# A two-layer backbone kernel: order of the convolutions, buffers of the last attention unit, loads of the keys and of x, sums of the out projection

## The chip, the cores and the metric

The kernel runs on one core of one Trainium2 chip. Its time is the device time of one execution in microseconds (us). The engines are named as the profile names them: PE is TensorE (PEld its weight loads), DVE is VectorE, ACT is ScalarE, POOL is GpSimd, SP is the engine that issues most DMAs (SPq is its queue). All data are fp32.

## The reference

2048 latent tokens and 256 context tokens of width 1024 go through two layers. Both have the same frame:

```python
for layer in range(2):
    shift, scale, gate = adaln(c, w_ada[layer], b_ada[layer])     # and the same of c_ctx for the context
    h = rms_norm(x, g) * (1 + scale) + shift
    p = h @ w_in[layer]                                            # split into the columns of the mixer
    y = even_mixer(p, ...) if layer == 0 else odd_mixer(p, ...)
    x = x + gate * (y @ w_out[layer])
```

Layer 0 has two branches, each multiplied by the SiLU of its own gate columns. One is global attention: 8 query heads and 2 key heads of size 64, rotary embedding, normalised queries and keys, every query against 256 + 2048 keys. The other is a Hyena convolution over columns `u`, three parts of 512 channels: a short convolution of 3 taps on each part, then twice a long convolution (by transforms along the tokens) and a product. The context tokens go through the same with their own keys only, and their result feeds layer 1.

Layer 1 has windowed attention (each block of 128 queries against three blocks of 128 keys and the context, with a sink) and neighbourhood attention (8 by 16 keys around each query on the 64-wide grid, with a bias table), again with gates. Only the latent tokens are returned.

## The kernel before

**Projections.** Each fp32 factor is split into a high and a low part, so a product is three matmuls for each 128 rows of the sum (`mm3`, L216 to L221), 24 for one output tile of 128x512. Weights come in tiles of 128x512 (256 KB): `load_w` (L230) issues the DMA into a ring of three buffers `wraw`, ScalarE casts the high part `whi` (L242), and GpSimd computes the low part `wlo` (L243), which frees the buffer. The 2304 tokens are taken in three groups of 768 (`GRP`; the context is in group 0). `Proj.rows` computes tiles with tokens on the partitions and hands each to an evacuation (`ev_q` and `ev_kv` normalise, rotate, transpose into `tq` and store to the DRAM tensor `qk`; `ev_v`, L348, copies into a tile `vt` and stores that). `Proj.cols` computes tiles with columns on the partitions, among them the gates.

**Layer 0 up to attention** (L1296 to L1345). The adaLN products of both layers are summed in three PSUM banks with the tag "x" (`ada_sum`), of which the last is copied out by `ada_gates` (L114). Then follow the projections of the token groups and, in `latent_conv` (L704), the short convolutions of parts 0 and 1 of `u`: loads of columns from DRAM, one ScalarE and two VectorE operations on each half (L724 to L726), transposes into tiles of tag "x", and for part 0 the first transform `hpA` (L668), in tiles of the same tag. `gate_convs` (L680) does the short convolution of part 2 with one ScalarE and two VectorE operations (L697) on each of 16 tiles. The order in the code is

```python
us((0, 1))
conv(0)
us((2,))
conv(1)
gates((0,))
gate_convs(...)
```

where `us` computes columns of `u` for the last token group.

**Attention** (`glob_attn`, L907) runs 16 units (a block of 512 queries and a pair of heads) of 9 batches of two key tiles each: scores (L979, L980), exponential on ScalarE (L981), sums of P by GpSimd (`pacc`, L993), values into `po` (L998); maxima of the scores (`pm`, `mx`, L892 and L893) run a unit ahead. TensorE's order is written out by hand in this part (`manual_schedule`); `hooks` puts the steps of the long convolution into the early batches, opens the pools of the out projection behind them (`out_pools`), and puts 18 jobs of the out projection into the later ones. A unit's end is `yo` (copy of `po`, L1064), and two batches later `finish` (L1000): load of the gates `agt`, sums `pd`, copy into `rec`, four reciprocals of a quarter each, two products on GpSimd (L1015, L1016), and `finish_y` (L365), which splits y into `yhi` and `ylo` and stores both to `yT`. All these tiles are in the attention's pool, which closes before the pools of layer 1's projection (`hT1`, `ips1`, `s1`) open.

**Out projection** (`out_jobs`, L1377). A job is one tile of 128 tokens by 512 columns: 6 of group 0 in both halves of the columns and 6 of group 1 in one half run in attention, 6 and 12 more before the projections of layer 1's groups 1 and 2. A job loads its weights (the first of a half), y (two tiles `oy`), and x (`ox`, 0.5 MB, once for the two halves), and ends with

```python
t = rg.tile([P, 512], F32, tag="bo", name="ot", bufs=3)
V.tensor_tensor(out=t, in0=po, in1=gate, op=ALU.mult)
V.tensor_tensor(out=x, in0=x, in1=t, op=ALU.add)
```

**Layer 1** (L1492 to L1516). For each group: its out projection, its norm (transposes `lnpt`, `lnh`, halves of `hT`), rows of window keys and values, window queries, neighbourhood keys, queries and values, and the gate columns. In the last group `window_keys` (L1440) is called between the window queries and the neighbourhood keys: five loads of keys and values for all tokens (`wk`, `wv`), 4.7 MB, into a pool that has just been opened.

**Order.** Outside the hand-ordered part a planner walks a simulated timeline and takes on each engine, among the instructions that are ready there, the one that comes first in the code. SP's DMA issues are one queue in that order, and a waiting issue holds up those behind it.

Of the kernel before, what the change touches and what calls it, by code (L numbers as in the profile page):

```python
# [9 lines left out]
F32 = mybir.dt.float32  # L10
# [30 lines left out]
def kern(ctx, tc, nc, I, C, out):  # L41
# [207 lines left out]
    class Proj:  # L249
# [98 lines left out]
        def ev_v(self, dst):  # L348
            def f(ps, tt):
                vt = self.rg.tile([P, 512], F32, tag="bo", name="vt", bufs=3)  # L350
                S.copy(vt, ps)
                nc.sync.dma_start(dst[tt], vt)
            return f
# [11 lines left out]
    def finish_y(sb, y, ft, t0, n, yT=yT, tags=("yhi", "ylo"), bufs=2, eng=None):  # L365

        hi = sb.tile([P, 512], F32R, tag=tags[0], name="yhi", bufs=bufs)
        lo = sb.tile([P, 512], F32R, tag=tags[1], name="ylo", bufs=bufs)
# [538 lines left out]
    def glob_attn(sb, ps, hooks, M0):  # L907
# [92 lines left out]
        def finish(n, yo, acc):  # L1000

            qb, hp = units[n]
            gt = sb.tile([P, 512], F32, tag="agt", name="agt", bufs=1)
# [4 lines left out]
            rec = sb.tile([P, 512], F32, tag="rec", name="rec", bufs=1)  # L1008
# [9 lines left out]
            return [lambda i=i: quarter(i) for i in range(0, 512, 128)] + [gate, lambda: finish_y(sb, yo, hp, qb * 512, 512, bufs=1, eng=G)]  # L1018
# [3 lines left out]
        acc, po, ended, last, pend = {}, {}, {}, None, []  # L1022
        total = 16 * 41
# [9 lines left out]
        for b in range(nb + 4):  # L1033
# [23 lines left out]
            if last is not None:  # L1057
# [5 lines left out]
                if ks == 16:  # L1063
                    yo = sb.tile([P, 512], F32, tag="yo", name="yo", bufs=2)  # L1064
# [144 lines left out]
    with stS as st:  # L1209
# [109 lines left out]
        us((0, 1))  # L1319
# [6 lines left out]
        conv(0)  # L1326
        us((2,))
        conv(1)
# [52 lines left out]
    def out_jobs(g, halves, xs=None, early=()):  # L1381
# [9 lines left out]
        def job(b, i, tt, mm):  # L1391
            c = slice(512 * b, 512 * b + 512)
            rg, xo, gl = O0["rg"], O0["xo"], O0["gl"]
            if i == 0 and w_out.get("b") != b:
# [4 lines left out]
            ty = [xo.tile([P, 8, P], F32R, tag=f"oy{s}", name=f"oy{s}", bufs=2) for s in range(2)]  # L1399
            for s in range(2):  # L1400
                nc.sync.dma_start(ty[s].bitcast(F32), yT[s, :, :, tt * P:(tt + 1) * P].rearrange("f p t -> p f t"))
# [9 lines left out]
            else:  # L1411
                if len(xs) == i:
                    xt = xo.tile([P, 1024], F32, tag="lnx", name="ox", bufs=6)
                    if early:
# [9 lines left out]
            t = rg.tile([P, 512], F32, tag="bo", name="ot", bufs=3)  # L1424
            V.tensor_tensor(out=t, in0=po, in1=gate, op=ALU.mult)
            V.tensor_tensor(out=x, in0=x, in1=t, op=ALU.add)
# [13 lines left out]
    def window_keys():  # L1440
# [8 lines left out]
        wvt = aw.tile([P, 18, P], F32, tag="wv", name="wv")  # L1449
        for s in range(2):  # L1450
# [21 lines left out]

# [505 lines left out]
```

## Time and profile before

| | |
|---|---|
| Median of 3 runs | 3856.79 us (3853.07 to 3857.14) |
| Profiled execution | 3855.73 us, span of the trace 3854.0 us |
| TensorE matmuls | 3628.1 us, 94% of the span |
| TensorE weight loads | 2607.1 us, 68% |
| VectorE, ScalarE, GpSimd | 2284.9, 1784.9, 1735.3 us (59%, 46%, 45%) |
| DMA | 586.23 MB, mean 152 GB/s |

The span is the time from the first to the last recorded instruction, here 1.7 us less than the time of the same execution. Matmuls of one engine overlap in their pipeline, so the durations of rows of TensorE may add up to more than the time they take. A row of the timeline is a run of like instructions on one engine; the bracket at its end is the idle time of that engine just before it, and what ended it. Times on the left are counted from the start of the span, and the layers' parts lie in it as follows: layer 0's projections and convolutions up to 1080 us, attention up to 2254 us, layer 1's projections up to about 3080 us, then layer 1's attentions.

### The profile page before, as it was taken

How to read it: one execution, taken by the hardware profiler on the slowest of the kernel's cores; microseconds unless marked ns; L12 is line 12 of the kernel's file. 1: busy time of each engine (PE TensorE's matmuls, PEld its weight loads, DVE VectorE, ACT ScalarE, POOL GpSimd, SP SyncE). 2: the span in 40 equal slices, each digit the busy share in tenths (PEclk: the TensorE clock that was granted, in tenths of full speed). 3: DMA queues.
4: the chain of work that ended last, by engine and by line, in shares of the span. 5: the costliest groups of instructions: out<-in, count | busy, mean ns of one | idle time of the engine just before them, and what ended most of it. 6: DMA issues, size and time to landing. Idle time of an engine off the chain costs nothing.

```text
span 3854.0 us, 57179 instructions
## 1 busy us (share of the span) xinstructions
PE 3628.1 (94%) x20112; PEld 2607.1 (68%) x20112; DVE 2284.9 (59%) x4370; ACT 1784.9 (46%) x3480; POOL 1735.3 (45%) x1433
## 2 busy tenths in 40 slices
PE   6999999999779999999989989999999999999999
PEld 2788777666555544555545667778877888888887
DVE  5854862634967765776664348185168167677622
ACT  3644642423526655666452334344144266666610
POOL 1544642222447786777796554353244123222310
PEclk8999999999889999999999999999999999999999
DMA  6343445366666555443253545545566376365365
GB/s 195 118 140 123 133 133 141 114 224 219 203 191 189 172 162 173 123 148 110 91 197 96 146 148 152 164 152 155 157 175 169 118 171 147 90 151 135 113 178 169
DMA packets 537650, 586.23 MB, mean 152 GB/s; under 512 B 70590, under 2 KB 361720, under 8 KB 534290
## 3 DMA queue, kind: packets, MB, share of 16 engines
q1 hardware_dynamic: 521090, 551.10, 48.8%
q10 hardware_dynamic: 13856, 25.18, 1.8%
q0 software_dynamic: 2416, 6.29, 0.6%
q8 instruction: 159, 2.61, 0.3%
q14 instruction: 129, 1.06, 0.1%
HBM read 389.62 MB, written 192.75 MB: 151 GB/s over the span
## 4 chain that ended last, share of the span: by engine, by line
PE 69%; DVE 13%; issue 5%; DMA 5%; ACT 4%; POOL 2%; SPq 1%; ACTq 0%; DVEq 0%; POOLq 0%
PE psB L221 16%; PE pso L221 7%; PE po L998 6%; PE psA L221 5%; PE npt L1580 4%; PE no L1592 4%; PE pS L979 4%; PE pm L892 3%; PE pS L980 3%; PE ns L1561 2%; PE ns L1567 2%; DMA wraw<-in_w_in_dram 2%; PE hpX L806 1%; PE hpC L799 1%; PE hpH L811 1%
## 5 line engine op out<-in xcount | busy, mean ns | idle before, releaser
L243 POOL TENSOR_TENSOR wlo<-wraw,whi 128x512 fp32r<-128x512 f32 x368 | 494.4, 1357 | 784.9 <-ACT whi L242 529.3
L993 POOL TENSOR_TENSOR pacc<-pacc,Pt 128x512 f32<-128x512 f32 x512 | 647.1, 1286 | 191.4 <-ACT Pt L981 189.1
L221 PE MATMUL psB<-hT,whi 128*128 128x512 f32 (+1 forms) x2560 | 659.4, 346 | 3.9 <-DVE bo L341 3.5
L221 PE MATMUL psA<-whi,hT 128*128 128x512 f32 (+1 forms) x1952 | 574.8, 375 | 28.3 <-ACT vt L361 8.4
L893 DVE TENSOR_REDUCE mx<-pm 128x1 f32<-128x512 f32 (+1 forms) x640 | 389.1, 631 | 194.4 <-PE pm L892 190.1
L221 PEld LDWEIGHTS psB<-hT,whi 128*128 128x128 f32 x2560 | 445.1, 190 | 87.0 <-issue 23.9
L981 ACT ACTIVATE Pt<-pS 128x512 f32<-128x512 f32 x576 | 333.0, 597 | 352.5 <-PE pS L980 313.7
L221 PE MATMUL psB<-hT,wlo 128*128 128x512 f32 (+1 forms) x1280 | 433.8, 344 | 0.0
L221 PEld LDWEIGHTS psA<-whi,hT 128*128 128x128 f32 x1952 | 359.0, 194 | 98.7 <-ACT vt L361 11.7
L242 ACT CAST whi<-wraw 128x512 fp32r<-128x512 f32 x368 | 222.2, 618 | 301.4 <-DMA wraw<-in_w_in_dram 119.5
L221 PE MATMUL psA<-wlo,hT 128*128 128x512 f32 (+1 forms) x976 | 358.3, 372 | 0.9 <-POOL wlo L243 0.8
L221 PE MATMUL pso<-whi,oy 128*128 128x512 f32 x1088 | 343.2, 394 | 7.9 <-DMA oy<-yT 7.0
L979 PE MATMUL pS<-Q,K 128*128 128x512 f32 x576 | 330.9, 574 | 15.3 <-ACT Pt L981 14.9
L998 PE MATMUL po<-Pt,V 128*64 128x512 f32 x1152 | 283.0, 613 | 0.0
L221 PEld LDWEIGHTS psB<-hT,wlo 128*128 128x128 f32 x1280 | 242.4, 190 | 41.1 <-issue 10.8
L1580 PE MATMUL npt<-ident,np 128*128 128x128 f32 x1488 | 258.6, 283 | 3.4 <-DVE ggt L1157 1.9
L979 PEld LDWEIGHTS pS<-Q,K 128*128 128x128 f32 x576 | 109.7, 190 | 208.7 <-issue 95.3
L221 PEld LDWEIGHTS pso<-whi,oy 128*128 128x128 f32 x1088 | 205.2, 189 | 59.0 <-DMA oy<-yT 7.0
L980 PE MATMUL pS<-Q,K 65*128 65x512 f32 x576 | 231.3, 402 | 10.9 <-DMA Q<-mr 10.9
L892 PE MATMUL pm<-K,Q 128*128 128x512 f32 x600 | 217.0, 384 | 16.6 <-DVE mx L893 16.5
L221 PE MATMUL pso<-wlo,oy 128*128 128x512 f32 x544 | 213.2, 394 | 1.2 <-POOL wlo L243 1.2
L221 PEld LDWEIGHTS psA<-wlo,hT 128*128 128x128 f32 x976 | 189.9, 195 | 32.4 <-POOL wlo L243 3.1
(345 smaller groups left out, 6490.8 us busy)
## 6 DMA issues: line engine op xcount, KB each, us to landing
wraw<-in_w_in_dram SPq DMA_DIRECT2D x312, 256.0 KB
oy<-yT SPq DMA_DIRECT2D x72, 512.0 KB
qk<-tq SPq DMA_DIRECT2D x50, 512.0 KB
fA<-fev SPq DMA_DIRECT2D x64, 256.0 KB
adaw<-in_w_ada_dram SPq DMA_DIRECT2D x32, 512.0 KB
hxb<-XA SPq DMA_DIRECT2D x64, 256.0 KB
hfb<-fA SPq DMA_DIRECT2D x64, 256.0 KB
XC<-hevc ACTq DMA_DIRECT2D x64, 256.0 KB
```

What stands on the lines that cost most here:

```text
L221: T.matmul(ps, a(x, kt), b(y, kt), start=(kt == 0 and n == 0), stop=(kt == 7 and n == 2))
L242: S.copy(hi, w)
L243: G.tensor_tensor(out=lo, in0=w, in1=hi.bitcast(F32), op=ALU.subtract)
L892: T.matmul(pm[:, :n], self.q1[:, h, qt * P:(qt + 1) * P], self.K1(c0, n), start=True, stop=True)
L893: V.tensor_reduce(out=self.mx[:, u, c:c + 1], in_=pm[:, :n], axis=AX.X, op=ALU.max)
L979: T.matmul(s, K1[kv][:, kt * P:(kt + 1) * P], q1[:, h, :], start=True, stop=False)
L980: T.matmul(s, K2[kv][:, kt * P:(kt + 1) * P], q2[:, h, :], start=False, stop=True)
L981: S.activation(pt[:, h, :], s, AF.Exp)
L993: G.tensor_tensor(out=acc[1][:, h], in0=acc[1][:, h], in1=p[:, h], op=ALU.add)
L998: T.matmul(po[64 * h:64 * h + 64, :], vt[:, kt, kv * 64:kv * 64 + 64], p[:, h, :], start=(kt == 0), stop=(kt == 17))
L1580: T.transpose(pt[:, i, :], self.p[h][:, (i0 + i) * P:(i0 + i + 1) * P], ident)
L1592: T.matmul(B["po"][64 * h:64 * h + 64, self.k, :], vt[:, kt, 64 * h:64 * h + 64], self.pT[h, i // 4][:, i % 4, :], start=(i == 0), stop=(i ...
```

## The change

Five edits. (1) `us((1,))` moves behind `conv(0)`, and `us((2,))` behind `conv(1)`. (2) For the last unit of attention (15), `agt`, `rec`, `yo`, `yhi` and `ylo` are taken from three tiles of the out projection's y ring (`last_home`), when the values of its last batch are done. (3) The five loads of window keys are issued after the rows of neighbourhood values, and held by copies of one column from the last `vt` into each of the three tiles. (4) A job's loads of y come ahead of its weights, and from the third job of group 0 on the load of x is held by a copy of one column from the x two jobs back. (5) The product with the gate is written back to the PSUM tile, and the sum with x reads it there; tile `t` goes.

```diff
         def ev_v(self, dst):
             def f(ps, tt):
-                vt = self.rg.tile([P, 512], F32, tag="bo", name="vt", bufs=3)
+                vt = self.late = self.rg.tile([P, 512], F32, tag="bo", name="vt", bufs=3)
                 S.copy(vt, ps)
                 nc.sync.dma_start(dst[tt], vt)
...
-    def finish_y(sb, y, ft, t0, n, yT=yT, tags=("yhi", "ylo"), bufs=2, eng=None):
-        hi = sb.tile([P, 512], F32R, tag=tags[0], name="yhi", bufs=bufs)
-        lo = sb.tile([P, 512], F32R, tag=tags[1], name="ylo", bufs=bufs)
+    def finish_y(sb, y, ft, t0, n, yT=yT, tags=("yhi", "ylo"), bufs=2, eng=None, home=None):
+        hi = home[0] if home else sb.tile([P, 512], F32R, tag=tags[0], name="yhi", bufs=bufs)
+        lo = home[1] if home else sb.tile([P, 512], F32R, tag=tags[1], name="ylo", bufs=bufs)
         S.copy(hi[:, :n], y)
         (eng or V).tensor_tensor(out=lo[:, :n], in0=y, in1=hi[:, :n].bitcast(F32), op=ALU.subtract)
...
-    def glob_attn(sb, ps, hooks, M0):
+    def glob_attn(sb, ps, hooks, M0, last_home):
...
         def finish(n, yo, acc):
             qb, hp = units[n]
-            gt = sb.tile([P, 512], F32, tag="agt", name="agt", bufs=1)
+            tail = iter(home[0]) if n == 15 else None
+            gt = next(tail) if tail else sb.tile([P, 512], F32, tag="agt", name="agt", bufs=1)
             nc.sync.dma_start(gt, g0[hp, :, qb * 512:qb * 512 + 512])
             pd = ps.tile([P, 512], F32, tag="m", name="pd", bufs=3)
             for h in range(2):
                 T.matmul(pd[64 * h:64 * h + 64, :], ones[:, 64:P], acc[:, h, :], start=True, stop=True)
-            rec = sb.tile([P, 512], F32, tag="rec", name="rec", bufs=1)
+            rec = next(tail) if tail else sb.tile([P, 512], F32, tag="rec", name="rec", bufs=1)
             S.copy(rec, pd)
             def quarter(i):
...
                 G.tensor_tensor(out=rec, in0=rec, in1=gt, op=ALU.mult)
                 G.tensor_tensor(out=yo, in0=yo, in1=rec, op=ALU.mult)
-            return [lambda i=i: quarter(i) for i in range(0, 512, 128)] + [gate, lambda: finish_y(sb, yo, hp, qb * 512, 512, bufs=1, eng=G)]
+            return [lambda i=i: quarter(i) for i in range(0, 512, 128)] + [gate, lambda: finish_y(sb, yo, hp, qb * 512, 512, bufs=1, eng=G, home=home[1] if tail else None)]
         acc, po, ended, last, pend = {}, {}, {}, None, []
+        home = []
...
                 for i in range(2):
                     values(m, ks + i, tiles[i], po[m])
                 if ks == 16:
-                    yo = sb.tile([P, 512], F32, tag="yo", name="yo", bufs=2)
+                    if m == 15:
+                        home[:] = last_home()
+                    yo = home[0].pop() if m == 15 else sb.tile([P, 512], F32, tag="yo", name="yo", bufs=2)
                     S.copy(yo, po.pop(m))
                     ended[b + 2] = m, yo
             if b in ended:
...
         xs2 = ln_in(GRP[2][0])
         gates()
         ln0(2, xs2)
-        us((0, 1))
+        us((0,))
         ls = s2.enter_context(tc.tile_pool(name="lc", bufs=1))
         def conv(part):
...
         conv(0)
+        us((1,))
+        conv(1)
         us((2,))
-        conv(1)
...
         def job(b, i, tt, mm):
             c = slice(512 * b, 512 * b + 512)
             rg, xo, gl = O0["rg"], O0["xo"], O0["gl"]
+            ty = [xo.tile([P, 8, P], F32R, tag=f"oy{s}", name=f"oy{s}", bufs=2) for s in range(2)]
+            for s in range(2):
+                nc.sync.dma_start(ty[s].bitcast(F32), yT[s, :, :, tt * P:(tt + 1) * P].rearrange("f p t -> p f t"))
             if i == 0 and w_out.get("b") != b:
                 w_out["b"] = b
                 w_out["w"] = load_w(I['w_out'][0][:, c], 512)
             if g == 0 and i == 0:
                 gate_half(gl[:, c], mm("pg"), 0, 0, b)
-            ty = [xo.tile([P, 8, P], F32R, tag=f"oy{s}", name=f"oy{s}", bufs=2) for s in range(2)]
-            for s in range(2):
-                nc.sync.dma_start(ty[s].bitcast(F32), yT[s, :, :, tt * P:(tt + 1) * P].rearrange("f p t -> p f t"))
             gate = gl[:, c]
             if tt == 16:
                 w_out["gc"] = rg.tile([P, 512], F32, tag="bo", name="gc", bufs=3)
...
             else:
                 if len(xs) == i:
                     xt = xo.tile([P, 1024], F32, tag="lnx", name="ox", bufs=6)
+                    if g == 0 and i > 1:
+                        V.tensor_copy(xt[:, 0:1], xs[i - 2][:, 0:1])
...
                 x = xs[i][:, c]
             po = mm("pso")
             mm3((po, lambda x, kt: ty[x][:, kt, :], lambda y, kt: w_out["w"][y][kt]))
-            t = rg.tile([P, 512], F32, tag="bo", name="ot", bufs=3)
-            V.tensor_tensor(out=t, in0=po, in1=gate, op=ALU.mult)
-            V.tensor_tensor(out=x, in0=x, in1=t, op=ALU.add)
+            V.tensor_tensor(out=po, in0=po, in1=gate, op=ALU.mult)
+            V.tensor_tensor(out=x, in0=po, in1=x, op=ALU.add)
             if tt < 16:
                 nc.sync.dma_start(rows(x1, tt)[:, c], x)
...
-    def window_keys():
+    def window_keys(late):
...
         wk1 = aw.tile([P, 2, 2304], F32R, tag="wk1", name="wk1")
         wk2 = aw.tile([P, 2304], F32R, tag="wk2", name="wk2")
         wvt = aw.tile([P, 18, P], F32, tag="wv", name="wv")
+        for t in (wk1[:, 0, 0:1], wk2[:, 0:1], wvt[:, 0, 0:1]):
+            V.tensor_copy(t, late[:, 0:1])
         for s in range(2):
             r = slice(64 * s, 64 * s + 64)
             nc.sync.dma_start(wk1[r].bitcast(F32), qk1[8:10, 0:64].rearrange("h p t -> p h t"))
...
             return [], [lambda: j(lambda nm: O0["ps"].tile([P, 512], F32, tag="s2", name=nm, bufs=2))], []
         return [], [], []
+    def last_home():
+        ty = [O0["xo"].tile([P, 8, P], (F32, F32, F32R)[i], tag=f"oy{i % 2}", name="yl", bufs=2).rearrange("p a b -> p (a b)") for i in range(3)]
+        return [ty[0][:, :512], ty[0][:, 512:], ty[1][:, :512]], (ty[2][:, :512], ty[2][:, 512:])
     HB, PB = 2, 5
     with tc.manual_schedule(engines={mybir.EngineType.PE}):
-        glob_attn(ga, gap, hooks, M0)
+        glob_attn(ga, gap, hooks, M0, last_home)
     for j in jobs:
         j(lambda nm: O0["ps"].tile([P, 512], F32, tag="s2", name=nm, bufs=2))
...
         pj.load_rope()
         pj.rows(512, 256, True, pj.ev_kv('win_k_norm', qk1[8:10], v1w))
         pj.rows(0, 512, False, pj.ev_q(lambda tt: qk1[0:8][:, :, tt * P:(tt + 1) * P], 'win_q_norm', -0.125, True))
-        if g == 2:
-            wm, sk, wk1, wk2, wvt = window_keys()
         pj.rows(1280, 512, True, pj.ev_q(lambda tt: qk1[18:26][:, :, tt * P:(tt + 1) * P], 'nat_k_norm', 1.0, False))
         pj.rows(768, 512, False, pj.ev_q(lambda tt: qk1[10:18][:, :, tt * P:(tt + 1) * P], 'nat_q_norm', -0.125, False))
         pj.rows(1792, 512, True, pj.ev_v(v1n))
+        if g == 2:
+            wm, sk, wk1, wk2, wvt = window_keys(pj.late)
         for b in range(2):
             pj.cols(2304 + 512 * b, True, g1[4 * b:4 * b + 4], False)
```

## Rows read from the trace of the kernel before

**Rows 1.** The page: busy time of each engine; shares of the chain that ended last.

```profile
PE 3628.1 (94%) x20112; PEld 2607.1 (68%) x20112; DVE 2284.9 (59%) x4370; ACT 1784.9 (46%) x3480; POOL 1735.3 (45%) x1433
...
PE 69%; DVE 13%; issue 5%; DMA 5%; ACT 4%; POOL 2%; SPq 1%; ACTq 0%; DVEq 0%; POOLq 0%
```

**Rows 2.** Stretches: us, length, busy PE PEld DVE ACT POOL, clock, DMA share, GB/s.

```profile
780.00:920.00 140.00, 140.00 (x676) 86.74 (x676) 34.78 (x42) 25.42 (x38) 34.56 (x24) 1.00 0.68 218
920.00:1080.00 160.00, 132.21 (x640) 99.21 (x640) 141.34 (x245) 83.00 (x159) 64.67 (x58) 0.88 0.66 207
2880.00:2920.00 40.00, 31.28 (x127) 23.83 (x126) 31.48 (x50) 13.85 (x28) 26.56 (x21) 0.87 0.77 191
2884.00:2902.00 18.00, 15.00 (x65) 10.80 (x63) 14.72 (x22) 4.79 (x10) 13.97 (x11) 1.00 0.98 202
3012.00:3079.00 67.00, 66.96 (x384) 58.36 (x382) 7.69 (x14) 14.88 (x28) 12.83 (x10) 1.00 0.32 100
```

**Rows 3.** Timeline, end of attention: start us, us, engine, line, operation, out<-in, count, [idle before].

```profile
2254.45 1.53 PE L302 MATMUL lnpt<-ident,ox 128*128 128x128 f32 x12 [0.68 <-ACT rec L1009]
2254.49 3.39 DVE L1012 RECIPROCAL rec<-rec 128x128 f32<-128x128 f32 x4 [10.62 <-ACT rec L1009]
2258.01 1.26 POOL L1015 TENSOR_TENSOR rec<-rec,agt 128x512 f32<-128x512 f32 x1 [5.37 <-issue]
...
2265.04 1.45 ACT L305 ACTIVATE lnh<-lnpt,gs 128x512 f32<-128x512 f32 x2 [3.77 <-DMA yT<-ylo]
...
2265.85 0.43 DVE L306 CAST hT<-lnh 128x512 fp32r<-128x512 f32 x1 [7.97 <-ACT lnh L305]
...
2265.87 1.11 PE L302 MATMUL lnpt<-ident,ox 128*128 128x128 f32 x4 [9.89 <-ACT lnh L305]
```

**Rows 4.** Timeline of attention with jobs of the out projection.

```profile
2037.61 24.73 POOL L993 TENSOR_TENSOR pacc<-pacc,Pt 128x512 f32<-128x512 f32 x20
...
2055.66 7.23 DVE L1426 TENSOR_TENSOR ox<-ox,ot 128x512 f32<-128x512 f32 x1
...
2063.55 0.39 PE L892 MATMUL pm<-K,Q 128*128 128x256 f32 x1 [4.35 <-DVE mx L893]
```

**Rows 5.** Instructions of a line: duration ns min/median/max, first and last start, forms.

```profile
L1426 DVE TENSOR_TENSOR ox<-ox,ot x30: 681/692/7231, 2055.7 to 2827.4; 128x512 f32<-128x512 f32 x30
...
L148 DVE TENSOR_TENSOR hpH<-hpH,cmt x64: 699/700/700, 1149.4 to 1801.7; 128x512 f32<-128x512 f32 x64
...
L149 DVE TENSOR_TENSOR hY<-hpH,cmW x64: 670/691/693, 1151.6 to 1802.5; 128x512 f32<-128x512 f32 x64
```

**Rows 6.** Timeline, the first jobs' loads in attention.

```profile
1995.37 3.73 SPq L1419 DMA_DIRECT2D ox<-in_x_dram  x3
...
2007.72 0.62 ACT L242 CAST whi<-wraw 128x512 fp32r<-128x512 f32 x1 [6.17 <-DMA wraw<-in_w_out_dram]
...
2008.89 0.80 PE L979 MATMUL pS<-Q,K 128*128 128x512 f32 x1 [6.18 <-ACT Pt L981]
```

**Rows 7.** Timeline of layer 1's projections, last token group.

```profile
2883.07 0.64 SPq L1452 DMA_DIRECT2D wk<-qk  x1
...
2904.85 0.58 ACT L212 CAST tq<-pt 64x512 fp32r<-64x512 f32 x1 [10.00 <-DMA qk<-tq]
...
2907.72 1.22 PE L221 MATMUL psA<-whi,hT 128*128 128x512 f32 x2 [6.80 <-ACT whi L242]
...
3012.35 0.58 ACT L351 COPY vt<-psA 128x512 f32<-128x512 f32 x1
...
3013.84 6.65 SPq L241 DMA_DIRECT2D wraw<-in_w_in_dram  x5
```

**Rows 8.** Timeline, the copy of the last adaLN sum out of PSUM.

```profile
921.70 0.58 ACT L114 COPY modM<-ada 64x512 f32<-64x512 f32 x1 [4.75 <-PE ada L95]
```

**Rows 9.** Instructions of a line, the short convolutions on VectorE.

```profile
L697 DVE SCALAR_TENSOR_TENSOR gy<-gu,cwx,gy x32: 734/750/1590, 927.4 to 1009.5; 128x512 f32<-128x512 f32 x32
...
L725 DVE SCALAR_TENSOR_TENSOR uy<-u,cwx,uy x16: 1269/1285/2324, 789.3 to 1061.3; 128x1024 f32<-128x1024 f32 x16
```

## The prediction

> **What bounds the kernel now.** I read the page's busy times first: TensorE is busy 94% of the span, and the chain that ended last runs 69% of the time on it [rows 1]. So an edit is worth the TensorE idle time that it removes, less what it adds. I then split the trace into stretches and looked in each, engine by engine, for what ended TensorE's long pauses. There are two kinds of stretch [rows 2]. In 780 to 920 us and in 3012 to 3079 us TensorE has no gap, so whatever is hidden there is free only while it stays small. In 920 to 1080 us, the convolutions, TensorE is idle 160 - 132.2 = 27.8 us, its clock is granted at 0.88, and VectorE is the full engine with 141.3 of 160 us. The remaining pauses that the change can touch are single gaps: 9.89 us where attention ends [rows 3], 4.35 us and 6.18 us near the end of attention [rows 4, 6], 6.80 us in the projection of the last token group [rows 7].
>
> **Closing tiles of unit 15 in another pool.** Now the next stage's first `lnh` on ScalarE waits 3.77 us for the landing of `yT<-ylo`, the last user of the attention pool, and TensorE stands from 2255.98 (2254.45 + 1.53) to 2265.87 [rows 3]. With `agt`, `rec`, `yo` and the two halves of y in the out projection's tiles, the attention pool is free when `rec` has been copied from `pd`, before 2254.45, where the transposes into PSUM already start. `lnh` can then start at once. What is late next is VectorE: the four reciprocals of unit 15 run from 2254.49 to 2257.88 and stand ahead of the first cast of hT, which now comes at 2265.85. So the stage moves up by 2265.85 - 2257.9 = 8.0 us. Above: 9.9 us, if the planner puts a cast between two reciprocals. Below: 5 us, if GpSimd's gating of unit 15 (from 2258.01, in 1.26 us steps) holds up the split of the next weights. The tiles are taken after the last of the 18 jobs, so no job's load waits for them. I take -8.0.
>
> **Out projection's sums in PSUM.** 36 jobs (18 in attention, 6 and 12 later) do two 128x512 operations each. The second, on SBUF alone, takes 692 ns as a median but once took 7231 ns [rows 5], from 2055.66 to 2062.89; GpSimd ran its `pacc` adds without a break from 2037.61 to 2062.34, and VectorE came free as that row ended. Behind it `mx` was late, and TensorE stood 4.35 us [rows 4]. The new forms are both in the trace: one that reads and writes the same PSUM tile takes 700 ns in every one of 64, one that reads PSUM and writes SBUF 691 ns and never above 693 ns, in 64 operations of the same attention loop [rows 5]. So the change costs 36 x (700 + 691 - 692 - 692) ns = 0.3 us of VectorE time, which hides behind the next job's 24 matmuls and would be 0.3 us on the path without them, and takes 6.5 us of one wait. On TensorE that is the 4.35 us; the rest was covered. Bounds: 0, if the same adds make ScalarE late instead, and -6.5. I take -4.3. A PSUM bank is held 0.7 us longer, behind 24 matmuls of another bank: nothing. [...]
>
> **Loads of x held, y before the weights.** The six loads of x (0.5 MB each) go out as the out projection's pools open, three of them right ahead of weight tile 4 of `w_out` [rows 6]. ScalarE's cast of that tile waits 6.17 us for its landing, with the exponentials of attention queued behind it, and TensorE stands 6.18 us. Held by a copy from the x two jobs back, four of the six loads leave the front of the queue; the copies themselves are four operations on one column. That takes up to 6.2 us. Against it, 1 MB of y now stands ahead of weight tile 1; at the 202 GB/s of [rows 2] this is 5 us that the first cast may wait, with the same exponentials behind it. SP's queue takes the held loads in order, so a `Q` load placed behind one would wait for a job; the jobs run on the same TensorE order, so I count nothing for it. Range -7 to +4; I take the middle, nearer the row that exists: -3.
>
> **Banded keys held back.** Now `wk` (3.5 MB) starts at 2883 in the middle of the projections [rows 7]. Stores of `tq` issued behind it land only when it is through: ScalarE waits 10.00 us for one, the weight casts stand behind that, and TensorE loses 6.80 us. The stretch 2880 to 2920 has a granted clock of 0.87 [rows 2], 10.4 us at the lower level, of which 3.6 us beyond the gap are matmuls at half speed: 1.8 us more. The change removes this: -8.6, rounded -9. But the loads do not vanish: they wait for the last `vt` of the last row block (3012.35 plus 0.58 = 3012.93), three one-column copies on an idle VectorE, and then five issues on SP [rows 7]. There they meet the gates' weights. The row of five weight issues begins at 3013.84, and its first two are tiles 7 and 8 of the gate now being multiplied, which need their buffers freed by a GpSimd split. The keys are ready before them and come earlier in program order, so I expect them ahead in SP's queue. The five loads are 4.7 MB with `wv`; at 202 GB/s [rows 2] they take 23.3 us, so tiles 7 and 8 land near 3041. The gates take 67 us for four pairs of column tiles of 512 tokens and four of 256 [rows 2], so 67 / 6 = 11.2 us for a pair of 512, and TensorE wants tile 7 three quarters into the first, near 3020.4. Bounds: 0, if SP has tiles 7 and 8 first, and 20 us of gap plus 2 of slow clock, if TensorE's order has nothing to put in between. The planner may put the next pair of columns there, three quarters of 11.2 us = 8.4 us. The nearest row is the collision itself, the same bytes against the same kind of traffic at 9 us, and I take that: +9, net 0.
>
> **Convolutions right behind their columns.** The order in the code changes, but the planner starts what is ready. The first part's VectorE work already begins at 789, right behind its own columns [rows 9]. Its next step then stands until 922.28, because the three PSUM banks that it shares are held by the adaLN sums until the copy of the last one ends there (921.70 + 0.58) [rows 8]. Nothing in the change moves that copy. Behind it VectorE has 141.3 us of work for 160 us [rows 2], the same work as before. So I take 0. Below: -18.7 us, all of VectorE's idle time in the stretch. Above: +24 us, the 32 operations of 750 ns of the gate convolutions [rows 9], if they lose their place (below).
>
> **The sum.** -8.0 - 4.3 - 3 + 0 + 0 = -15.3 us against the profiled execution's own 3855.73 us (span 3854.0 and 1.7 around it): 3840.4. That execution lies 1.1 us under the median of the three runs, so 3841.5 on their scale; I say 3841.
>
> **Rivals.**
> 1. The keys find room. If the two weight tiles go first, or TensorE fills the wait, the 9 us gained stay: 3841 - 9 = 3832. For it: the stretch of the gates moves only 100 GB/s [rows 2]. Against it: five loads issue faster than GpSimd frees a buffer.
> 2. The keys cost their full price, 22 us against 9 gained: 3841 + 13 = 3854, no change. For it: nothing issued behind `wk` landed before it [rows 7]. Against it: other matmuls are ready.
> 3. Slower: the last third of u falls behind. Its columns now come after the second convolution in the code; if TensorE does them after the release of the banks instead of before it, the gate convolutions that read them lose the stretch from 927 to 1010 in which they fill VectorE's gaps, and their 24 us come at the end of the full engine: 3841 + 24 = 3865. It decides from the point where the last eviction of u passes the release of the banks at 921.70. Against it: TensorE has nothing else ready before that.
> 4. The new order does pack VectorE, -18.7 us: 3822. For it: VectorE is busy only 34.8 of the 140 us before 920 [rows 2]. Against it: the banks.
>
> **How the numbers follow.** Forecast 0.40 (own range 3833 to 3849), rival 1 0.20, rival 2 0.20, rival 3 0.12, rival 4 0.08. About 0.2%, 7.7 us, is what a measurement of this kernel can tell from no change: 3849 and 3864 are the bounds around the median. Faster: 0.38 of the forecast, rivals 1 and 4, and 0.02 of rival 2: 0.68. Slower: 0.08 of rival 3 and 0.02 of rival 2. The rest, 0.22, is the same. The range runs from 3818, below rival 4 with a small further gain left out, to 3863, which leaves out most of rival 3.
>
> **What would show it.** Closing tiles: no wait for `yT<-ylo` before `lnh`, first hT cast 2 to 4 us after the reciprocals start. Sums: every operation of the out projection under 0.75 us, no 4 us wait for `mx`. Loads of x: fewer than three `ox` issues before weight tile 4, no cast waiting 6 us. Keys: no 10 us wait for `tq`, and a gap of TensorE some 9 us after the first gate matmul, ended by a weight cast; without this gap the forecast is wrong to the fast side. Convolutions: first `hpA` still right behind the copy of the adaLN sums, and the stretch to the first attention matmul within 5 us of its length; if it is 10 us shorter or longer, my reading of the banks is wrong.

## The result: 0.82% faster, and the profile after

The changed kernel takes 3822.98 us (median of 4 runs, 3819.43 to 3829.62) against 3855.57 us before (4 runs). The ratio is 0.9918, 95% interval 0.9901 to 0.9935, which is 25 to 38 us of 3857 and 31.6 at its middle. The forecast was 3841, 15 us faster: the sign was right, the gain came out twice as large, outside the forecast's own range (3833 to 3849) and inside the whole one (3818 to 3863). The profiled execution of after is the slowest of its four (3829.62 us, span 3827.7), so the trace shows some 26 us, not 32. Before the first changed instruction of attention it is 2.6 us late against the trace of before; the length of the conv stage agrees within 0.2 us.

The page of after, as in [rows 1]; then its stretches, as in [rows 2] (the third and fourth are the old stretches 2880 to 2920 and 3012 to 3079, moved by what had been gained until then):

```profile
PE 3626.5 (95%) x20112; PEld 2605.8 (68%) x20112; DVE 2266.1 (59%) x4377; ACT 1784.6 (47%) x3480; POOL 1735.0 (45%) x1433
...
PE 68%; DVE 13%; issue 6%; DMA 5%; ACT 4%; POOL 2%; SPq 1%; ACTq 0%; DVEq 0%; POOLq 0%; another core or an unknown queue 0%
```

```profile
780.00:920.00 140.00, 140.00 (x682) 87.12 (x681) 33.58 (x44) 25.59 (x38) 34.84 (x24) 1.00 0.68 218
920.00:1080.00 160.00, 131.93 (x640) 99.24 (x639) 141.07 (x246) 82.36 (x157) 63.84 (x57) 0.87 0.66 208
...
2852.00:2892.00 40.00, 38.75 (x173) 29.84 (x172) 35.74 (x65) 15.19 (x33) 32.02 (x24) 1.00 0.41 113
2984.00:3051.00 67.00, 66.00 (x376) 57.45 (x375) 7.96 (x17) 13.90 (x26) 12.79 (x10) 1.00 0.63 167
```

The first two rows are those of before to about 1 us on every engine: the new order of the convolutions moved nothing. In the third TensorE is idle 1.3 us instead of 8.7 and the clock is whole. The fourth was to lose 9 us to the key loads and lost 1.0.

The timeline of after, as in [rows 3, 6, 7]: the first weight tiles of the out projection, the end of attention, and the keys.

```profile
1997.93 0.62 ACT L242 CAST whi<-wraw 128x512 fp32r<-128x512 f32 x1 [2.19 <-DMA wraw<-in_w_out_dram]
...
2000.10 0.50 PE L979 MATMUL pS<-Q,K 128*128 128x512 f32 x1 [2.53 <-ACT Pt L981]
...
2242.10 3.39 DVE L1013 RECIPROCAL yl<-yl 128x128 f32<-128x128 f32 x4 [10.53 <-ACT yl L1010]
...
2243.52 1.45 ACT L305 ACTIVATE lnh<-lnpt,gs 128x512 f32<-128x512 f32 x2
...
2247.31 0.35 DVE L274 TENSOR_SCALAR gwin_q_norm<-gwin_q_norm 128x64 f32<-128x64 f32 x1 [1.82 <-DMA gnat_k_norm<-in_nat_k_norm_dram]
2247.58 0.41 DVE L306 CAST hT<-lnh 128x512 fp32r<-128x512 f32 x1
...
2248.05 0.58 PE L221 MATMUL psA<-whi,hT 128*128 128x256 f32 x1 [2.37 <-DVE hT L306]
...
2985.15 0.61 SPq L1460 DMA_DIRECT2D wk<-qk  x1
...
2988.68 0.74 SPq L1462 DMA_DIRECT2D wv<-v1w  x1
...
3010.39 1.29 ACT L242 CAST whi<-wraw 128x512 fp32r<-128x512 f32 x2 [13.86 <-DMA wraw<-in_w_in_dram]
```

`lnh` no longer waits for a store, the keys stand in SP's queue where the forecast had them, and weight tiles 7 and 8 of the gate are late (13.86 us on ScalarE): the step was right up to the point where TensorE should have noticed.

The out projection's second operation, as in [rows 4, 5], from the forms of its line and the timeline:

```profile
L1432 DVE TENSOR_TENSOR ox<-pso,ox x30: 679/691/692, 2051.6 to 2806.0; 128x512 f32<-128x512 f32 x30
```

```profile
2032.24 19.93 POOL L993 TENSOR_TENSOR pacc<-pacc,Pt 128x512 f32<-128x512 f32 x16
...
2051.62 0.68 DVE L1432 TENSOR_TENSOR ox<-pso,ox 128x512 f32<-128x512 f32 x1
```

GpSimd's adds run without a break as before, and none of these operations takes over 0.7 us. Their median from PSUM is 691 ns, that of the old form 692 [rows 5]: on the median the new form is no dearer.

### The profile page after: what moved, and what is told of

Its sections match the earlier page's. It is cut to its first block, busy times and chain, and to the rows that moved or that the text cites. A ratio compares the mean times of both kernels' runs of the same rounds, so it can differ in the third digit from the quotient of the medians.

```text
span 3827.7 us, 57198 instructions
## 1 busy us (share of the span) xinstructions
PE 3626.5 (95%) x20112; PEld 2605.8 (68%) x20112; DVE 2266.1 (59%) x4377; ACT 1784.6 (47%) x3480; POOL 1735.0 (45%) x1433
## 4 chain that ended last, share of the span: by engine, by line
PE 68%; DVE 13%; issue 6%; DMA 5%; ACT 4%; POOL 2%; SPq 1%; ACTq 0%; DVEq 0%; POOLq 0%; another core or an unknown queue 0%
PE psB L221 16%; PE pso L221 7%; PE po L998 7%; PE npt L1593 4%; PE psA L221 4%; PE no L1605 4%; PE pS L979 4%; PE pm L892 3%; PE pS L980 3%; PE ns L1574 2%; PE ns L1580 2%; DVE tq L213 2%; PE hpX L806 1%; PE hpC L799 1%; PE hpH L811 1%
```

## The experiments

Gains are given as (1 - ratio) x 3857 us, with the interval where the argument rests on it. e1 to e5 do one edit each on the kernel before; e6 to e8 and e10 alter the changed kernel, e9 alters e6, e11 and e12 alter e9. A ratio is against runs of the kernel before that were taken together with that run; their medians went from 3855.6 to 3859.6 us, so medians of rows that were not taken together compare only to about 4 us.

| run | what | median us | ratio (95%) | gain us |
|---|---|---|---|---|
| e1 | closing tiles alone | 3845.48 | 0.9973 (0.9961 to 0.9986) | 10.4 (5.4 to 15.0) |
| e2 | sums from PSUM alone | 3847.43 | 0.9979 (0.9970 to 0.9988) | 8.1 (4.6 to 11.6) |
| e3 | loads of x and y alone | 3849.99 | 0.9985 (0.9976 to 0.9993) | 5.8 (2.7 to 9.3) |
| e4 | banded keys alone | 3852.36 | 0.9990 (0.9981 to 0.9998) | 3.9 (0.8 to 7.3) |
| e5 | order alone | 3856.54 | 0.9992 (0.9983 to 1.0001) | 3.1 (-0.4 to 6.6) |
| e6 | layer 1's adaLN behind the convolutions | 3824.91 | 0.9913 (0.9899 to 0.9926) | 33.6 |
| e7 | x not held | 3822.74 | 0.9906 (0.9890 to 0.9921) | 36.3 |
| e8 | y first in group 0 only | 3821.29 | 0.9904 (0.9891 to 0.9918) | 37.0 |
| e9 | e6, gate convolutions ahead of adaLN | 3790.87 | 0.9822 (0.9809 to 0.9835) | 68.7 (63.6 to 73.7) |
| e10 | keys at the new place, not held | 3825.86 | 0.9916 (0.9902 to 0.9929) | 32.4 |
| e11 | e9 in the old order | 3826.11 | 0.9919 (0.9904 to 0.9933) | 31.2 |
| e12 | e9 with e8 | 3788.80 | 0.9820 (0.9806 to 0.9834) | 69.4 (64.0 to 74.8) |

e1 to e5 add up to 31.3 us, the whole change to 31.6. The five intervals together leave some 8 us either way, and within that the parts neither help nor hinder each other.

**e1, closing tiles.**

```diff
-                    yo = sb.tile([P, 512], F32, tag="yo", name="yo", bufs=2)
+                    if m == 15:
+                        home[:] = last_home()
+                    yo = home[0].pop() if m == 15 else sb.tile([P, 512], F32, tag="yo", name="yo", bufs=2)
...
+            rec = next(tail) if tail else sb.tile([P, 512], F32, tag="rec", name="rec", bufs=1)
```

> The kernel before with the closing tiles of unit 15 alone taken from the out projection's tiles. Theory (each edit removes its own gap of TensorE, and the parts add up): the 9.89 us gap at the first lnh is gone, at most 2.5 us are left for the first cast of hT behind the four reciprocals, and the kernel is 7 to 10 us faster, 3846 to 3849 us. Rival (what is gained at the end of attention comes back in the projection behind it, because GpSimd's gating of unit 15 now stands between the splits of the next weights): 3 to 5 us faster at most, with new gaps of 1 us and more in the 100 us behind attention that end on GpSimd's wlo.

In place of the 9.89 us gap two are left, 0.71 and 2.42 us. The rival's new gaps behind it did not come; the opposite did: TensorE's waits for VectorE's `qn` some 100 us later shrink. Between the same two matmuls (from 2345.82 on in before, from 2342.23 on in e1):

```profile
2345.82:2420.60 74.78, 67.03 (x297) 53.11 (x296) 52.80 (x95) 28.98 (x57) 20.23 (x16) 0.98 0.53 155
```

```profile
2342.23:2410.59 68.36, 65.60 (x298) 51.79 (x297) 45.67 (x95) 28.96 (x57) 21.40 (x16) 1.00 0.57 169
```

TensorE is idle 7.75 us there before and 2.76 in e1. This is no accident of one execution: the same stretch takes 74.7 to 75.0 us in all five traces with the old closing tiles and 68.1 to 68.5 in all nine with the new ones. The theory holds.

**e2, sums from PSUM.**

```diff
-            t = rg.tile([P, 512], F32, tag="bo", name="ot", bufs=3)
-            V.tensor_tensor(out=t, in0=po, in1=gate, op=ALU.mult)
-            V.tensor_tensor(out=x, in0=x, in1=t, op=ALU.add)
+            V.tensor_tensor(out=po, in0=po, in1=gate, op=ALU.mult)
+            V.tensor_tensor(out=x, in0=po, in1=x, op=ALU.add)
```

> The kernel before with the out projection's products left in PSUM. Theory (only an operation of VectorE on SBUF alone is held up by GpSimd's unbroken run of pacc adds): no operation of the out projection's two lines over 0.75 us, the 4.35 us gap before pm is gone, and the kernel is 4 to 8 us faster, 3848 to 3852 us. Rival (another engine is late in the same place, or the long operation was an accident of one execution): within 2 us of the kernel before, or a gap of the same size elsewhere between 2040 and 2080.

That the long operation was an accident is refuted by the kernels that kept the old form. The forms of the line in e2, then in e3 and in e4:

```profile
L1425 DVE TENSOR_TENSOR ox<-pso,ox x30: 680/691/692, 2054.0 to 2816.7; 128x512 f32<-128x512 f32 x30
```

```profile
L1428 DVE TENSOR_TENSOR ox<-ox,ot x30: 680/693/7247, 2049.9 to 2826.4; 128x512 f32<-128x512 f32 x30
```

```profile
L1426 DVE TENSOR_TENSOR ox<-ox,ot x30: 681/693/7272, 2051.4 to 2826.4; 128x512 f32<-128x512 f32 x30
```

Three traces of the old form, with [rows 5], hold one operation each for 7.23, 7.25 and 7.27 us (e1 and e5 as well, 7.23 each); both of the new form hold none. The product, which reads one operand from PSUM, was never held in either form: 0.69 us at most in before, 0.70 in after.

**e3, loads.**

```diff
+            ty = [xo.tile([P, 8, P], F32R, tag=f"oy{s}", name=f"oy{s}", bufs=2) for s in range(2)]
...
             if i == 0 and w_out.get("b") != b:
...
+                    if g == 0 and i > 1:
+                        V.tensor_copy(xt[:, 0:1], xs[i - 2][:, 0:1])
```

> The kernel before with y loaded ahead of the weights and four loads of x held. Theory (the wait for weight tile 4 goes and no other takes its place): the gap of 6.18 us near 2003 shrinks to 2.5 us or less, the kernel is 4 to 7 us faster, 3849 to 3852 us. Rival (1 MB of y ahead of weight tile 1 costs up to 5 us elsewhere): within 2 us of the kernel before.

The gap is 3.42 us (I had said 2.5 or less), the gain as the theory said. The length of this one gap is a poor measure, though: in e4, which has the old loads, it is 3.48 us. The stretch around it is steady. Between the same two matmuls, 1977.05 and 2043.62 in before, it takes 66.0 to 67.4 us in the five traces with the old loads, e4 among them, and 58.3 in e3.

**e4, keys.**

```diff
-        if g == 2:
-            wm, sk, wk1, wk2, wvt = window_keys()
...
         pj.rows(1792, 512, True, pj.ev_v(v1n))
+        if g == 2:
+            wm, sk, wk1, wk2, wvt = window_keys(pj.late)
```

> The kernel before with the banded keys alone moved behind the neighbourhood values and held. My forecast: 9 us gained near 2900, 9 us given back in the gates, net 0 (3854 to 3858 us). Theory after the first result: tiles 7 and 8 of the gate's weights do land late, ScalarE waits more than 10 us for them, but TensorE has other column tiles with the first six weight tiles in five PSUM banks and loses under 2 us: 5 to 8 us faster, 3848 to 3851 us.

In the trace TensorE's lead over before grows from 0.5 us (the same matmul at 2880.33 instead of 2880.86) to 7.6 at the last `vt` (3004.75 instead of 3012.35), and 1.5 are given back in the gates; ScalarE waits 14.19 us there for tiles 7 and 8. The gain, 3.9 us, lies just under the 5 to 8 expected, and its interval, 0.8 to 7.3, takes in most of that. Net zero is out, by little in the times and clearly in the trace.

**e5, order.**

```diff
-        us((0, 1))
+        us((0,))
         conv(0)
+        us((1,))
+        conv(1)
         us((2,))
-        conv(1)
```

> The kernel before with the order of the convolutions and the columns of u alone changed. Theory (the planner already starts each convolution right behind its columns, and the adaLN sums hold the three PSUM banks until about 922): first hpA within 1 us of the end of that copy, the stretch from 780 to 1127 unchanged within 3 us, the kernel within 4 us of the kernel before. Rival (the third part of u falls behind, or VectorE is packed better): 10 to 24 us to either side in that stretch.

First `hpA` at 921.4, straight behind the copy of the adaLN sums; from there to the first score matmul 204.4 us, before 204.5. The theory holds for the kernel as it was. The next runs ask about the banks.

**e6, adaLN of layer 1 behind the convolutions.** Only `ada_gates` of layer 0 stays ahead of them.

```diff
-        head = ada_head(1, fs, "s", 3)
-        ada_sum(pa[:2], head[1], 0, lambda kt: ada_rows(1, kt, [ada_w() for _ in range(3)]))
...
         us((2,))
+        pa = [xp.tile([P, 512], F32, tag="x", name=f"ada{i}", bufs=3) for i in range(2)]
+        head = ada_head(1, fs, "s", 3)
+        ada_sum(pa, head[1], 0, lambda kt: ada_rows(1, kt, [ada_w() for _ in range(3)]))
...
         s2.close()
```

> The changed kernel with the adaLN sums of layer 1 (16 us of DMA or more for each 3 MB of weights, two PSUM banks) moved behind the convolutions and the last columns of u. Theory (the banks hold up the convolutions, and VectorE has 105 of 140 us idle before 920): first hpA at least 60 us earlier, and up to 18.7 us, VectorE's idle time in 920 to 1080, gained: 3804 to 3820 us. Rival (the banks are not what holds it, or the 12.6 MB of weights, behind the convolutions, put the same time into the stretch before attention): first hpA moves, and the kernel is not faster than the changed one, 3820 to 3845 us.

The 16 us for each 3 MB are what the 191 GB/s of [rows 2] give (15.7 us); in before the 24 loads, 12.6 MB, were issued within 98 us (814.6 to 912.7). Both were half right. The banks did hold the convolutions: first `hpA` came at 816.9, 106 us earlier than before, and the first score matmul 21 us earlier. (e6 moves the sums' banks and the loads of their weights together; that it was the banks is read from before and e5, where `hpA` starts right behind the copy that frees the last one.) And the kernel is no faster, since the first step of the long convolution still comes at 1141.9. The forms of two lines and the timeline of e6 say why:

```profile
L668 PE MATMUL hpA<-zst,dAh x32: 387/397/505, 816.9 to 901.0; 128*128 128x512 f32 x32
...
L697 DVE SCALAR_TENSOR_TENSOR gy<-gu,cwx,gy x32: 730/750/753, 1059.2 to 1132.3; 128x512 f32<-128x512 f32 x32
```

```profile
1141.88 2.04 PE L806 MATMUL hpX<-hxb,hdB 128*128 128x512 f32 x2 [26.60 <-DMA hdC<-in_dftC_const]
```

The gate convolutions ran from 927 to 1010 before [rows 9] and from 1059 to 1132 here: their buffers open only when the adaLN's pool closes, and the long convolution's loads stand behind them.

**e7, x not held.**

```diff
-                    if g == 0 and i > 1:
-                        V.tensor_copy(xt[:, 0:1], xs[i - 2][:, 0:1])
```

> The changed kernel without the copies that hold the loads of x; y still ahead of the weights. Theory (the hold is what lets the weights through): the gap near 2000 is 6 us or more again, 5 to 9 us slower than the changed kernel, 3828 to 3832 us. Rival (the order of y and weights did it): the gap stays at 2.5 to 3.5 us and the time within 2 us of the changed kernel's 3823.

```profile
1999.10 0.50 PE L979 MATMUL pS<-Q,K 128*128 128x512 f32 x1 [3.01 <-ACT Pt L981]
```

The rival is right as far as the time tells. The five loads of x go out ahead of weight tile 4 as before, and the gap is half as long. The stretch around it, between the same two matmuls in before, in after and in e7:

```profile
1977.05:2043.62 66.57, 53.89 (x199) 27.51 (x198) 32.06 (x50) 27.83 (x50) 57.59 (x48) 0.90 0.51 159
```

```profile
1980.85:2039.54 58.69, 52.92 (x200) 26.64 (x199) 30.36 (x50) 26.86 (x50) 56.34 (x47) 0.94 0.47 144
```

```profile
1978.12:2039.03 60.91, 53.26 (x200) 26.56 (x198) 32.08 (x50) 28.20 (x50) 57.61 (x48) 0.92 0.55 174
```

Of the 7.9 us that this stretch lost, 5.7 are lost without the hold; the other 2 may be the hold's, but the time of e7 does not show them. With y first, weight tiles 4 to 6 come later in the planner's order, and ScalarE has their casts behind the exponentials instead of ahead of them.

**e8, y first in group 0 only.** The same lines stand ahead of the weights under `if g == 0:` and behind them under `if g:`.

> The changed kernel with y ahead of the weights in the jobs of group 0 only, and the old order in the jobs of groups 1 and 2. Theory (y ahead of the weights costs 2 to 4 us where the out projection of group 2 runs alone): the stretch from the first to the last job of group 2 is 2 to 4 us shorter, 3819 to 3821 us. Rival (that stretch varies by itself): no difference in it beyond 1 us, 3822 to 3824 us.

The theory is not shown: the stretch of group 2's jobs is 76.9 us, 78.0 in the changed kernel, but 75.9 and 76.1 in e10 and e7 and 80.1 in e3, which have y first everywhere. It varies by itself, as the rival says, and the intervals of e8 and of the changed kernel overlap.

**e9, gate convolutions ahead of the adaLN.**

```diff
+        s3 = ExitStack()
-        ls = s2.enter_context(tc.tile_pool(name="lc", bufs=1))
+        ls = s3.enter_context(tc.tile_pool(name="lc", bufs=1))
...
         us((2,))
+        s3.close()
+        with tc.tile_pool(name="gc", bufs=1) as gc:
+            gate_convs(gc, range(4))
         pa = [xp.tile([P, 512], F32, tag="x", name=f"ada{i}", bufs=3) for i in range(2)]
```

> The changed kernel with the adaLN sums of layer 1 behind the convolutions as in e6, and the gate convolutions moved ahead of these sums, in the buffers that the convolutions leave, so that they no longer wait for the sums' pool to close. Theory (in e6 the 22 us gained before attention were lost to the gate convolutions, which start only when that pool closes, and behind which the buffers of the long convolution open): the last gate convolution ends before 1060, the gap of 26.6 us before hpX shrinks below 8 us, and the kernel is 12 to 22 us faster than the changed one: 3801 to 3811 us. Rival (the weights' DMA, 12.6 MB, is what delays hpX): the gap stays above 20 us, 3820 to 3826 us.

32 us faster than the changed kernel by the medians (3822.98 - 3790.87), 37 by the ratios, and beyond the 12 to 22 expected either way. Stretches of e9, then its forms and its timeline:

```profile
780.00:920.00 140.00, 139.22 (x712) 100.64 (x711) 90.09 (x109) 61.38 (x93) 48.31 (x24) 1.00 0.70 228
920.00:1080.00 160.00, 153.61 (x801) 105.97 (x800) 100.99 (x189) 58.46 (x121) 66.60 (x70) 0.98 0.79 239
```

```profile
L697 DVE SCALAR_TENSOR_TENSOR gy<-gu,cwx,gy x32: 702/945/1845, 958.0 to 1047.9; 128x512 f32<-128x512 f32 x32
```

```profile
1109.57 0.77 PE L980 MATMUL pS<-Q,K 65*128 65x512 f32 x1 [4.63 <-DMA Q<-mr]
...
1113.80 1.91 PE L806 MATMUL hpX<-hxb,hdB 128*128 128x512 f32 x2
```

VectorE has 90 us of work before 920 instead of 34, and 101 instead of 141 behind it; TensorE's idle time from 920 to 1080 falls from 28 to 6.4 us and its clock rises from 0.87 to 0.98. The bound of 18.7 us, VectorE's idle time behind 920, had taken for granted that its 141 us stay there; 40 of them moved ahead of 920, so it was no bound. The gap before `hpX` is gone as well.

**e10, keys not held.**

```diff
-        for t in (wk1[:, 0, 0:1], wk2[:, 0:1], wvt[:, 0, 0:1]):
-            V.tensor_copy(t, late[:, 0:1])
```

> The changed kernel with the key loads at their new place in the code, but without the three copies that hold them. Theory (the planner issues what is ready: without the hold the loads go out as soon as the stores of the last keys are through, near 2870 to 2900, and the old collision is back): a wait of 6 us and more on a load or store of that stretch, 3 to 7 us slower than the changed kernel, 3826 to 3830 us. Rival (the place in the code is enough): the loads start at 2975 or later and the time is within 2 us of the changed kernel's 3823.

```profile
2853.57 0.64 SPq L1458 DMA_DIRECT2D wk<-qk  x1
...
2875.26 0.58 ACT L212 CAST tq<-pt 64x512 fp32r<-64x512 f32 x1 [9.53 <-DMA qk<-tq]
...
2878.11 1.22 PE L221 MATMUL psA<-whi,hT 128*128 128x512 f32 x2 [6.27 <-ACT whi L242]
```

The loads go out where they did before the edit, and the old wait and the old gap are back: the copies do the work, not the place in the code. The times of e10 and of the changed kernel can't be told apart, so the 4 us of this edit are shown by e4 and by the gap, not by this ratio.

**e11, e9 in the old order.**

```diff
-        us((0,))
+        us((0, 1))
...
         conv(0)
-        us((1,))
-        conv(1)
         us((2,))
+        conv(1)
```

> The kernel of e9 with the old order of the convolutions and the columns of u. Theory (the order is worth nothing because the planner starts what is ready, with or without the banks): within 3 us of e9's 3791, first hpA within 3 us of 822. Rival (with the banks free the order decides, since now each convolution can start behind its own columns): the second part's columns and convolutions move by 20 us or more, and the kernel is 5 us or more slower than e9.

The theory fails, and the rival holds: 35 us slower than e9 (3826.11 - 3790.87), 37 by the ratios. The first `hpA` comes at 835.5, not at 822. The last transpose of the convolutions is at 983 instead of 948, the last adaLN product at 1116 instead of 1078, and behind them stand the key maxima of attention, in the same PSUM tag as the adaLN sums. Timeline of e11:

```profile
1105.17 1.92 PE L95 MATMUL ada<-adaw,sil 128*32 128x512 f32 x4 [7.41 <-DMA adaw<-in_w_ada_dram]
...
1117.44 20.98 PE L892 MATMUL pm<-K,K 128*128 128x512 f32 x38 [0.68 <-ACT modM L114]
```

So the order is worth nothing while the banks are held (e5) and 35 us in e9, where they are not and the sums with their loads stand behind the convolutions. Which of the two moves of columns does it was not tried.

**e12, both.** The kernel of e9 with the edit of e8.

> The kernel of e9 with the loads of y as in e8 (ahead of the weights in the jobs of group 0 only). Theory (the two gains lie in different stretches and add up): 2 to 4 us faster than e9, 3787 to 3789 us. Rival (y's place varies with the run): 3790 to 3793 us.

3788.8 us against 3790.9, well inside both intervals: nothing to be told.

## Why the prediction was right, and where its sizes were off

**Right in its range partly by luck.** 3823 us is 10 us outside the forecast's own range and 9 us below rival 1. It lies in the whole range only because rival 4 (VectorE packed better by the new order, 3822) had opened it downward to 3818, and what rival 4 describes did not happen: the stretch of the convolutions kept its length. By the middles of the intervals the sum came out short in each of its five terms.

**The gaps were the right ones.** Of the four that the prediction named, 4.35 and 6.80 us went, and 9.89 and 6.18 gave way to shorter ones, each by the edit that it named; the effects add up within their intervals. The signs that held: `lnh` at once, no operation over 0.75 us, fewer loads of x before weight tile 4, no 10 us wait for `tq`, `hpA` behind the adaLN copy. Two signs failed: the first cast of hT came 5.5 us after the reciprocals' start, not 2 to 4, and the gap that the keys were to cost did not come, which the prediction itself had called the sign of being wrong to the fast side.

**Sums: 4.3 forecast, 8.1 measured.** The step took the gap's own length. What it left out is the row behind it. Stretches of before, the gap and what follows it, then what follows the three other gaps that were named, with the 6.80 us gap itself:

```profile
2059.20:2063.55 4.35, 0.01 (x2) 0.00 (x1) 4.35 (x3) 0.60 (x1) 3.14 (x3) 1.00 0.02 4
2063.55:2067.30 3.75, 3.75 (x10) 2.98 (x11) 1.47 (x3) 0.00 (x0) 0.00 (x0) 0.54 0.19 70
2265.87:2270.00 4.13, 4.13 (x25) 4.13 (x26) 1.43 (x3) 2.84 (x5) 2.88 (x3) 0.67 0.31 88
2900.90:2907.70 6.80, 0.02 (x1) 0.00 (x0) 2.14 (x5) 1.89 (x4) 1.09 (x1) 0.69 0.91 283
2907.70:2911.50 3.80, 3.78 (x9) 3.01 (x10) 3.70 (x4) 1.82 (x3) 3.75 (x4) 0.50 0.75 209
2008.89:2012.60 3.71, 3.71 (x8) 2.11 (x10) 1.38 (x2) 2.64 (x5) 3.24 (x3) 0.50 0.28 87
```

In the 3.7 to 4.1 us behind each of these four gaps TensorE is busy and the granted clock is 0.50 to 0.67. By single microseconds of these stretches it reads 0.50 or 1.00, and a value between only where it changes; a matmul of 128x512 starts every 0.43 us at 0.50 (2908.74 to 2913.01) and every 0.23 us at 1.00 (2889.71 to 2893.68). So 0.50 is the lower level here. For the sums that is 3.75 x 0.46 = 1.7 us. A second operation on SBUF alone was held for 1.72 us at 2129.87, and the gap behind it shrank from 2.29 to 1.25. 4.35 + 1.7 + 1.0 = 7.1, of 7.9 seen in e2's trace (its lead over before grows from 1.7 to 9.6 us between 2057 and 2250). The prediction had counted this slow clock for the keys and for no other gap, and there too low: it took all of the 6.80 us as slow, while the clock over the gap is 0.69, which is 4.2 us at the lower level. Of its 10.4 us, 6.2 lie behind the gap, not 3.6, and cost 3.1 us, not 1.8.

**Loads: 3 forecast, 5.8 measured.** The middle of -7 and +4 was taken. The wait for weight tile 4 went whole, and the +4 (y ahead of weight tile 1) came in part: the 2.53 us gap of after stands where ScalarE waits 2.19 us for weight tile 2, whose load now goes out behind y, with an exponential behind the casts. Between the two matmuls of e7's stretches TensorE's idle time fell from 12.7 to 5.8 us, and the stretch by 7.9. The step's reason was mostly wrong: not the hold (some 2 us of the stretch, e7) but where ScalarE's casts stand. The 7.9 us lie within the interval of e3's 5.8 (2.7 to 9.3).

**Closing tiles: 8.0 forecast, 10.4 measured (5.4 to 15.0).** The first cast of hT came not at the end of the reciprocals (2242.10 + 3.39 = 2245.49) but at 2247.58, since VectorE's queue stood 1.82 us in the scaling of a norm's gain (`gwin_q_norm`) that waited for a DMA. So the place itself gave 9.89 - 0.71 - 2.37 = 6.8 us; the rest came from the `qn` gaps 100 us later (6.4 us of stretch in e1), which nothing in the prediction foresaw. Together that is 13.2 us, as in e1's trace (3.3 us behind the trace of before at 2252, 10.0 ahead at 2421), and within the interval of the times. Short gaps were followed by a slow clock too, 0.50 and 0.62 in two of three places. Stretches of after, behind this gap and behind the 2.53 us one at the weights, and of before, behind the 2.29 us gap at 2130.52, where the clock stayed whole:

```profile
2248.05:2252.00 3.95, 3.95 (x17) 3.78 (x18) 1.73 (x4) 1.03 (x2) 1.78 (x2) 0.50 0.36 116
2000.10:2004.00 3.90, 3.90 (x11) 2.12 (x13) 1.98 (x3) 0.44 (x1) 3.90 (x4) 0.62 1.13 340
```

```profile
2132.81:2137.00 4.19, 4.19 (x18) 2.35 (x19) 0.28 (x1) 0.60 (x1) 2.67 (x4) 1.00 0.47 140
```

**Keys: 0 forecast, 3.9 measured.** The failing term is the +9 given back. The tiles were as late as worked out; but the price of 9 us was taken from the old collision, where TensorE stood 6.80 us. Here it had other matmuls with the six tiles that were there, as the step itself had thought possible, stayed busy through ScalarE's wait and was idle 1.0 us (rival 1, by its second condition).

**Order: 0 forecast, 3.1 measured (-0.4 to 6.6, so no change is not out).** The reading of the banks was right (e5, e6), the general reason beside it ("the planner starts what is ready") was not: with the banks free, the order decides 35 us (e11).

## What to carry to other kernels

Price a gap of TensorE by its length and by the slow rows behind it: here a gap of 4 us cost 6; a gap of 2 to 3 us had slow rows behind it in some places and none in others. Before an edit that reorders work is called worthless or good, look for what holds the first step of the moved work; here three PSUM banks made an order worth nothing that is worth 35 us once a 12.6 MB side job stands behind it, and the side job's pool then has to be kept off the next user's path. A load for which ScalarE waited 14 us cost TensorE 1 us here, because it had other tiles open.

## What was not expected of the hardware

VectorE's operations on SBUF alone were held here while GpSimd worked, short ones too: 1.01 to 1.22 us against 0.17. Timeline of before, four operations on 128x8 elements, of which the last shows what one takes when nothing stands in the way, 0.17 us:

```profile
2396.31 3.77 POOL L243 TENSOR_TENSOR wlo<-wraw,whi 128x512 fp32r<-128x512 f32 x3 [4.01 <-ACT whi L242]
...
2396.61 1.01 DVE L121 TENSOR_TENSOR rsq<-ss,rs 128x8 f32<-128x8 f32 x1
2397.66 1.22 DVE L122 TENSOR_TENSOR rsq<-rsq,rs 128x8 f32<-128x8 f32 x1
2398.91 1.20 DVE L123 TENSOR_SCALAR rsq<-rsq 128x8 f32<-128x8 f32 x1
2400.14 0.17 DVE L124 TENSOR_TENSOR rs<-rs,rsq 128x8 f32<-128x8 f32 x1
```

The three long ones end at 2397.62, 2398.88 and 2400.11, just as GpSimd's three (1.26 us each from 2396.31) do; the next takes 0.17. This ended in a 2.68 us gap of TensorE at 2399. No operation of the form that reads PSUM was held: 0.69 us at most in after, also at 2051.62 beside GpSimd's adds. The hold at 2056 was longer than one instruction of GpSimd: 7.23 us are over five of its adds of 1.24 us (24.73 / 20 [rows 4]). What holds VectorE was not shown. Why VectorE got in between instructions at 2397 and not at 2056 was not tried and stays open.
